# Operand building of each token in three steps, woven around the next token's normalisation

## The chip, the cores and the metric

The kernel runs on one core of a Trainium2 chip. The metric is the device time of one execution in microseconds, the median over several runs. The kernel before took 969.36 us (three runs, 968.85 to 971.9). The engines are TensorE (PE, its weight loads PEld), VectorE (DVE), ScalarE (ACT), GpSimd (POOL) and SyncE (SP), which issues most DMAs. Each engine works through its own list in order.

## The reference

One encoder layer over 768 tokens (a sequence of 512 and one of 256) of width 1024, all in float32. The part around the change is this:

```python
mix = jnp.concatenate([y_rg, y_ml], axis=-1).astype(x.dtype)
x = x + jnp.matmul(mix, w_out)
h = rmsnorm(x, norm2_g)              # y = x * rsqrt(mean(x*x) + EPS) * g
uv = dwconv(jnp.matmul(h, w_up), ffn_conv_w, ffn_conv_b, FFN_CONV // 2, FFN_CONV // 2)
gate, val = jnp.split(uv, 2, axis=-1)
x = x + jnp.matmul(jax.nn.gelu(gate) * val, w_down)
```

Ahead of it come an RMSNorm, the input projection, a gated linear recurrence (channels 0 to 511 of `mix`) and an mLSTM (channels 512 to 1023); behind it only the final RMSNorm.

## The kernel before

Every large product is computed from high and low parts: an operand is rounded to the matmul's format (high), the residue is kept (low), and three matmuls are summed: high times high, low times high, high times low. ScalarE writes the high parts by a copy, VectorE or GpSimd the low ones by a subtraction.

The 768 tokens are six tiles of 128, here called tokens 0 to 5. The output projection is done in two halves of the contraction. The first half (lines 856 to 864) uses the recurrence's channels and adds into `x2`, two tiles of 512 columns per token. The second half is the loop over `PTOK` = 0, 3, 1, 4, 2, 5 at lines 1046 to 1065, which the change rewrites. One pass does, for token c:

1. twelve matmuls for columns 0 to 511 of the projection (`mm_list`, four k-slices times three parts) into a PSUM bank of tag b;
2. `evac`: VectorE adds the bank to `x2`; `square`: ScalarE squares the result and sums each row;
3. `mix_T` for the next token: four transposes into a bank of tag c, a ScalarE copy (`mth`) and a VectorE subtraction (`mtl`);
4. `early`: a piece of preparing the first up-projection weights (`hi_g`, `pair`, `lo_g0`);
5. twelve matmuls for columns 512 to 1023; after the eighth of them `norm2_back` of the token of the pass before: eight transposes of its normalised rows `xn` into two banks of tag c, and the building of operands from them;
6. `evac` and `square` for the second half, then `norm2_front`: `tok_rstd` (a ScalarE Sqrt and small VectorE operations) and two VectorE operations that write `xn` = x times rstd times `g2p`. `g2p` is the gain vector, held in two PSUM banks of tag g;
7. `x2_spill`: the token's rows go to DRAM, on SP's queue.

The up-projection is done by a seven-product scheme on 2 by 2 blocks (Strassen's, in Winograd's form): tokens 0 to 2 against tokens 3 to 5, first against second half of the width. So operand building needs token c - 3 when it comes to token c. For tokens 0 to 2, `norm2_back` writes operands 1 and 2 and keeps two copies `xq`. For tokens 3 to 5 it also forms t1 to t3 on VectorE (two of them read PSUM), t4 on GpSimd, and the high and low parts of operands 3 to 7 (`put_hi` on ScalarE; `put_lo` on GpSimd, or mostly on VectorE for the very last token, whose `norm2_back` is called at line 1215 after the third product). `put_hi(4)` reads t4.

All five engines run in the order of the program in this stage (lines 67 and 868), so where a call stands decides what stands behind it in an engine's list. The tiles `xn`, `xq`, `tq`, `sq`, `mth`, `mtl`, `x2` and the mLSTM's `h` share one pool of 22 slots (`stile`, line 554). The PSUM pool of the stage has tags g (two banks), c (three) and b (three), laid out in the order of their first use; the next pool, `ps8`, has five banks b and three banks c, and its first product is `prod(bd, w, 7, ...)` at line 1212. A tile of a new pool waits for the tiles that had its place (`reuse_waits="tile"`).

After the stage, `window` runs 23 times over up-projection, convolution and gating, and then comes the down-projection.

Of the kernel before, what the change touches and what calls it, by code (L numbers as in the profile page):

```python
# [15 lines left out]
P = 128  # L16
# [17 lines left out]
def kernel(  # L34
# [519 lines left out]
    def stile(name):  # L554
        return mlp["p"].tile([P, 516], F32, tag="s", name=name)
# [279 lines left out]
    def square(c, i, xx, n, j_):  # L835
        if i == 0:
            sums[c] = tiny.tile([P, 4], F32, tag="s2", name="s2")
        A.activation(j_[:, 0:n], xx, AF.Square, accum_out=sums[c][:, i : i + 1])  # L838
# [3 lines left out]
    def tok_rstd(c):  # L842
        s2 = sums.pop(c)
        pre = tiny.tile([P, 3], F32, tag="pre", name="pre")
        V.tensor_scalar(pre[:, 0:1], s2[:, 0:1], 1.0 / D, EPS, op0=MUL, op1=ADD)
        last = s2[:, 1:2]
        rt = tiny.tile([P, 3], F32, tag="rt", name="rt")
        A.activation(rt[:, 0:1], last, AF.Sqrt, bias=pre[:, 0:1], scale=1.0 / D)
        V.tensor_scalar(pre[:, 2:3], last, 1.0 / D, pre[:, 0:1], op0=MUL, op1=ADD)
        V.tensor_scalar(pre[:, 2:3], pre[:, 2:3], -0.5, None, op0=MUL)  # L850
        V.reciprocal(rt[:, 1:2], rt[:, 0:1])
        V.tensor_scalar(rt[:, 2:3], rt[:, 1:2], rt[:, 1:2], pre[:, 2:3], op0=MUL, op1=MUL)
        V.tensor_scalar(rt[:, 0:1], rt[:, 2:3], 1.5, rt[:, 1:2], op0=ADD, op1=MUL)
        return rt[:, 0:1]
# [20 lines left out]
    def bank():  # L875
        return pm["p"].tile([P, 512], F32, tag="b", name="b", bufs=pm["b"])

    def cbank(name):
        return pm["p"].tile([P, 512], F32, tag="c", name=name, bufs=3)
# [70 lines left out]
    def put_hi(i, o, x):  # L950
        A.activation(r32(hilo(i, o)[0]), quad(x), AF.Copy)  # L951

    def put_lo(i, o, x, eng):
        hi, lo = hilo(i, o)
        eng.tensor_tensor(r32(lo), quad(x), hi, op=SUB)

    def mix_T(c):
        ps = cbank("mt")
        for h in range(4):
            PE.transpose(ps[:, h * P : (h + 1) * P], hml[c][:, h * P : (h + 1) * P], ident[:])  # L960
        th, tl = stile("mth"), stile("mtl")
        A.activation(r32(th[:, 0:512]), ps[:], AF.Copy)
        V.tensor_tensor(r32(tl[:, 0:512]), ps[:], th[:, 0:512], op=SUB)
        return th, tl
# [2 lines left out]
    gb = rawtile("g2b")  # L967
    nc.sync.dma_start(gb[:, 0:D], g2.to_broadcast([P, D]))
    sets[0].load_v()
    gbp = [pm["p"].tile([P, 512], F32, tag="g", name="g2p", bufs=2) for _ in range(2)]  # L970
    for hf in range(2):
        A.activation(gbp[hf][:], gb[:, hf * 512 : hf * 512 + 512], AF.Copy)

    def norm2_front(c):
        rr = tok_rstd(c)
        xs = []
        for hf in range(2):
            xn = stile("xn")
            V.scalar_tensor_tensor(xn[:, 0:512], x2[c][hf][:, 0:512], rr, gbp[hf][:], op0=MUL, op1=MUL)  # L979
            xs.append(xn)  # L980
        return xs

    def x2_spill(c):
        for hf in range(2):
# [1 line left out]

    xq = {}

    def norm2_back(c, xs):
        ps = []  # L990
        for hf in range(2):
            ps.append(cbank("tr"))
            for h in range(4):
                PE.transpose(ps[hf][:, h * P : (h + 1) * P], xs[hf][:, h * P : (h + 1) * P], ident[:])
        if c < 3:
            xq[c] = [stile("xq"), stile("xq")]
            for hf in range(2):
                put_hi(1 + hf, c * P, ps[hf])
            put_lo(1, c * P, ps[0], V)
            A.activation(xq[c][1][:, 0:512], ps[1][:], AF.Copy)  # L1000
            A.activation(xq[c][0][:, 0:512], ps[0][:], AF.Copy)
            put_lo(2, c * P, xq[c][1], G)
            return
        o = (c - 3) * P
        x11, x21 = xq.pop(c - 3)
        p12, p22 = ps
        x22 = stile("xq")
        t1, t2, t3, t4 = (stile("tq")[:, 0:512] for _ in range(4))
        A.activation(x22[:, 0:512], p22[:], AF.Copy)
        V.tensor_tensor(t1, p12[:], x11[:, 0:512], op=SUB)  # L1010
        V.tensor_tensor(t3, x22[:, 0:512], p12[:], op=SUB)
        V.tensor_tensor(t2, p22[:], t1, op=SUB)
        put_hi(5, o, t1)
        put_hi(7, o, t3)
        put_hi(6, o, t2)
        put_hi(3, o, p22)
        if c == PTOK[-1]:
            put_lo(5, o, t1, V)
            put_lo(7, o, t3, V)
            put_lo(6, o, t2, V)  # L1020
            V.tensor_tensor(t4, x21[:, 0:512], t2, op=SUB)
            put_hi(4, o, t4)
            put_lo(3, o, p22, V)
            put_lo(4, o, t4, G)
        else:
            put_lo(3, o, x22, G)
            G.tensor_tensor(t4, x21[:, 0:512], t2, op=SUB)
            put_hi(4, o, t4)
            for i, t in ((5, t1), (7, t3), (6, t2), (4, t4)):
                put_lo(i, o, t, G)  # L1030

    def mm_list(ps, acts, hf):
        n = [0]
        for k in range(4):
            (ah, al), (wh, wl) = acts[k], us[k]
            for i, (a, w) in enumerate(((ah, wh), (al, wh), (ah, wl))):
                PE.matmul(ps[:, 0:512], lhsT=a, rhs=w[:, hf * 512 : hf * 512 + 512],  # L1037
                          start=k == 0 and i == 0, stop=k == 3 and i == 2)
                yield

    mt = {PTOK[0]: mix_T(PTOK[0])}
    fr = {}
    u0 = sets[0]
    early = {0: lambda: (u0.hi_g(), u0.sums()), 1: lambda: (u0.pair(0),), 2: lambda: (u0.pair(1),),
             3: lambda: (u0.lo_g0(),), 4: lambda: (), 5: lambda: ()}
    for n, c in enumerate(PTOK):
        th, tl = mt.pop(c)
        acts = [(r32(th[:, i * P : i * P + P]), r32(tl[:, i * P : i * P + P])) for i in range(4)]
        ps = bank()
        for _ in mm_list(ps, acts, 0):  # L1050
            pass
        square(c, 0, evac(c, 0, ps), 512, stile("sq"))
        if n + 1 < NT:
            mt[PTOK[n + 1]] = mix_T(PTOK[n + 1])
        early[n]()
        ps = bank()
        for q, _ in enumerate(mm_list(ps, acts, 1)):
            if q == 7 and n:
                norm2_back(PTOK[n - 1], fr.pop(PTOK[n - 1]))
        square(c, 1, evac(c, 1, ps), 512, stile("sq"))  # L1060
        fr[c] = norm2_front(c)
        if n:
            x2_spill(PTOK[n - 1])
        if n == 4:
            sets[1] = UpSet(1)
# [146 lines left out]
    prod(bd, w, 7, True, 0, cut)  # L1212
    prod(ba, w, 1)
    prod(bb, w, 6, True, 0, cut)
    norm2_back(PTOK[-1], fr.pop(PTOK[-1]))
    u0.hi_22()
    u0.lo_22()()
    mlstack.close()
# [204 lines left out]
```

## Time and profile before

| | |
|---|---|
| median of three runs | 969.36 us |
| the profiled execution | 970.04 us, span 968.3 us |
| PE busy / PEld busy | 95% / 86% of the span |
| VectorE, ScalarE, GpSimd busy | 65%, 52%, 42% |
| granted TensorE clock, mean | 0.978 |
| chain that ended last | PE 73%, DVE 15%, ACT 4%, issue 3%, POOL 3%, DMA 2% |

The profile also cuts the span into 40 slices of 24.2 us. A digit is the busy share of a slice in tenths; PEclk is the granted TensorE clock in tenths:

```profile
PE   8897999999898998799999999999999899999997
POOL 4621433266453326396676676676672000010001
PEclk9898999999999898899999999999999999999999
```

The loop over the six tokens runs from 337 to 393 us of the span, slices 13 to 16 counted from 0, and the first products follow it. From slice 18 on TensorE is busy in nearly all of every slice. The lists of the engines and the waits between them are read from the trace in the section on the rows.

### The profile page before, as it was taken

Reading aid. Unit: us, or ns where it says so; the run is one execution under the profiler, and the core shown is the slowest. Engines: PE = TensorE matmul, PEld = TensorE weight load, DVE = VectorE, ACT = ScalarE, POOL = GpSimd, SP = SyncE. Lnnn points to the kernel's source line nnn. Section 1 sums busy time; section 2 is a strip of 40 time slices with the busy share of each in tenths; the row PEclk is TensorE's granted clock in tenths of the full one; section 3 lists DMA queues with packets and bytes.
Section 4 is the critical chain, followed back from the end, with each engine's and each line's share of the span. In section 5 each row is a group of like instructions: output and inputs, shape, how many; then the busy total and the mean of one; then the engine's idle time right before and its main releaser. Section 6 shows DMA issues by size and latency. Waiting matters only on the chain.

```text
span 968.3 us, 13652 instructions
## 1 busy us (share of the span) xinstructions
PE 916.3 (95%) x5066; PEld 835.3 (86%) x5066; DVE 631.4 (65%) x1176; ACT 500.3 (52%) x826; POOL 404.1 (42%) x261
## 2 busy tenths in 40 slices
PE   8897999999898998799999999999999899999997
PEld 7796877898897776799999999999999788888885
DVE  7678999437869554567667667667677664346523
ACT  6463565154454154476657657667565453326523
POOL 4621433266453326396676676676672000010001
PEclk9898999999999898899999999999999999999999
DMA  6411111042335112142232232331321596527811
GB/s 223 143 56 45 44 66 44 18 149 88 88 104 200 45 56 76 44 148 92 89 120 80 101 120 68 113 120 60 120 77 47 196 344 245 171 82 264 312 40 66
DMA packets 42419, 110.47 MB, mean 114 GB/s; under 512 B 4976, under 2 KB 12656, under 8 KB 42352
## 3 DMA queue, kind: packets, MB, share of 16 engines
q1 hardware_dynamic: 40320, 106.38, 32.5%
q10 hardware_dynamic: 2032, 3.22, 0.9%
q8 instruction: 40, 0.66, 0.3%
q14 instruction: 27, 0.22, 0.1%
HBM read 93.78 MB, written 15.79 MB: 113 GB/s over the span
## 4 chain that ended last, share of the span: by engine, by line
PE 73%; DVE 15%; ACT 4%; issue 3%; POOL 3%; DMA 2%; SPq 0%; POOLq 0%; ACTq 0%; DVEq 0%
PE b L1080 34%; PE d L1313 20%; PE big L141 6%; PE sm L832 3%; PE sm L742 3%; PE sm L451 2%; DVE xc L350 1%; PE b L1037 1%; POOL w_lo L107 1%; DVE thi L386 1%; DVE xgl L252 1%; DMA w_raw<-in_w_down_dram 1%; DVE rs L199 1%; DVE nt L197 1%; ACT hq L951 1%
## 5 line engine op out<-in xcount | busy, mean ns | idle before, releaser
L1080 PE MATMUL b<-hq,w_sh 128*128 128x384 f32 (+2 forms) x792 | 200.1, 335 | 4.4 <-DVE xn L979 3.5
L1313 PE MATMUL d<-w_hi,act 128*128 128x512 f32 x576 | 181.0, 396 | 2.9 <-DVE vl L1126 2.0
L925 POOL TENSOR_TENSOR w_sl<-w_S,w_sh 128x1024 fp32r<-128x1024 f32 x48 | 115.6, 2409 | 120.1 <-ACT w_sh L924 120.1
L1080 PEld LDWEIGHTS b<-hq,w_sh 128*128 128x128 f32 x792 | 143.3, 189 | 5.2 <-issue 4.0
L1313 PEld LDWEIGHTS d<-w_hi,act 128*128 128x128 f32 x576 | 108.6, 189 | 29.0 <-DVE vl L1126 2.5
L1080 PE MATMUL b<-hq,w_sl 128*128 128x384 f32 (+2 forms) x396 | 132.4, 334 | 0.0
L106 ACT ACTIVATE w_hi<-w_raw 128x1024 fp32r<-128x1024 f32 (+1 forms) x77 | 81.0, 1056 | 94.2 <-PE d L1313 57.0
L107 POOL TENSOR_TENSOR w_lo<-w_raw,w_hi 128x1024 fp32r<-128x1024 f32 (+1 forms) x29 | 74.9, 2592 | 122.4 <-ACT w_hi L106 74.9
L1313 PE MATMUL d<-w_lo,act 128*128 128x512 f32 x288 | 113.4, 394 | 0.0
L1080 PE MATMUL b<-hq,w_gh 128*128 128x384 f32 x384 | 98.7, 338 | 0.0
L1289 POOL TENSOR_TENSOR z<-xr,fgb 128x512 f32<-128x512 f32 x6 | 7.8, 1294 | 215.2 <-ACT sq L838 128.4
L107 DVE TENSOR_TENSOR w_lo<-w_raw,w_hi 128x1024 fp32r<-128x1024 f32 x48 | 58.8, 1225 | 58.5 <-ACT w_hi L106 56.9
L1080 PEld LDWEIGHTS b<-hq,w_sl 128*128 128x128 f32 x396 | 75.0, 189 | 0.0
L1080 PEld LDWEIGHTS b<-hq,w_gh 128*128 128x128 f32 x384 | 69.9, 188 | 0.0
L1313 PEld LDWEIGHTS d<-w_lo,act 128*128 128x128 f32 x288 | 54.5, 189 | 12.3
L1080 PE MATMUL b<-hq,w_gl 128*128 128x384 f32 x192 | 64.8, 338 | 0.0
L1108 ACT ACTIVATE cv<-vl,col 128x512 f32<-128x512 f32 (+1 forms) x48 | 32.1, 669 | 49.1 <-DVE vl L1204 47.9
L141 PE MATMUL big<-xgh,w_hi 128*128 128x512 f32 x208 | 54.8, 344 | 2.5 <-DVE kT L762 2.3
L1080 PE MATMUL b<-hq,w_v 128*128 128x384 f32 x288 | 54.4, 337 | 1.0 <-DVE wv L1235 1.0
L141 PE MATMUL big<-xgl,w_hi 128*128 128x512 f32 x208 | 53.3, 337 | 0.0
L141 PE MATMUL big<-xgh,w_lo 128*128 128x512 f32 x208 | 53.3, 337 | 0.0
L1080 PEld LDWEIGHTS b<-hq,w_v 128*128 128x128 f32 x288 | 50.7, 188 | 1.1 <-ACT w_gh L906 1.1
(299 smaller groups left out, 2068.6 us busy)
## 6 DMA issues: line engine op xcount, KB each, us to landing
w_raw<-in_w_down_dram SPq DMA_DIRECT2D x48, 512.0 KB, 4.4
w_g<-in_w_up_dram SPq DMA_DIRECT2D x24, 512.0 KB, 4.1
w_v<-in_w_up_dram SPq DMA_DIRECT2D x24, 512.0 KB, 4.9
actd<-vl SPq DMA_DIRECT2D x24, 384.0 KB, 2.6
a_raw<-actd SPq DMA_DIRECT2D x48, 192.0 KB, 4.5
w_raw<-in_w_fm_dram SPq DMA_DIRECT2D x13, 512.0 KB, 3.4
w_raw<-in_w_out_dram SPq DMA_DIRECT2D x8, 512.0 KB, 5.4
M<-md SPq DMA_DIRECT2D x12, 256.0 KB, 4.2
```

What stands on the lines that cost most here:

```text
L106: A.activation(r32(hi), raw[:, 0:n], AF.Copy)
L107: (V if key[0] == "down" else G).tensor_tensor(r32(lo), raw[:, 0:n], hi, op=SUB)
L141: PE.matmul(dst, lhsT=w, rhs=x[:, lo:hi], start=first and i == 0, stop=last and i == 2,)
L197: V.tensor_tensor(t[:], y, y, op=MUL)
L199: V.scalar_tensor_tensor(y, t[:], 1.5, y, op0=ADD, op1=MUL)
L451: PE.matmul(ps[:, 0:n], lhsT=x[:, p0 : p0 + P], rhs=w[:, o : o + n], start=k == 0 and i == 0, stop=k == 7 and i == 2)
L742: PE.matmul(ps[:, 0:256], lhsT=x[:, p0 : p0 + P], rhs=w[:, o : o + 256], start=n == 0, stop=n == 23)
L832: PE.matmul(ps[:, 0:512], lhsT=a, rhs=w[:, hf * 512 : hf * 512 + 512], start=first and k == 0 and i == 0, stop=last and k == n - 1 and i == 2)
L925: G.tensor_tensor(r32(sl[:, 0:1024]), x, sh[:, 0:1024], op=SUB)
L1080: PE.matmul(t[:, a:b], lhsT=wt, rhs=r32(hq[:, k, off + a : off + b]), start=first and n == 0, stop=n == len(seq) - 1, skip_group_check=True)
L1108: A.activation(t[:, 0 : hi - lo], x[:, lo:hi], AF.Identity, bias=fb[:, m : m + 1], scale=fw[:, 48 + m : 49 + m])
L1313: PE.matmul(bk[c, hf], lhsT=r32(x[:, c * P : c * P + P]), rhs=w[:, hf * 512 : hf * 512 + 512], start=k == 0 and i == 0, stop=k == 23 and i ...
```

## The change

`norm2_front` goes into the loop, and `norm2_back` is split into `norm2_T` (the transposes) and two generators, `back_a` for tokens 0 to 2 and `back_b` for tokens 3 to 5. A generator is advanced in steps: once before the second `evac`, once after the second `square`, and to its end after `xn` is written. The transposes come after ten matmuls of the second half (after eight in the last pass) in place of eight. `mix_T` of the next token moves ahead of the first `square`. Among GpSimd's residues the one of operand 3 moves from ahead of t4 to the end. A bank of tag b is taken first, then `mix_T` takes tag c, and the copies into `g2p` (tag g) follow; an extra one-column Sqrt on ScalarE stands behind them.

```diff
-    gbp = [pm["p"].tile([P, 512], F32, tag="g", name="g2p", bufs=2) for _ in range(2)]
-    for hf in range(2):
-        A.activation(gbp[hf][:], gb[:, hf * 512 : hf * 512 + 512], AF.Copy)
...
+    def norm2_T(c, xs):
         ps = []
         for hf in range(2):
             ps.append(cbank("tr"))
             for h in range(4):
                 PE.transpose(ps[hf][:, h * P : (h + 1) * P], xs[hf][:, h * P : (h + 1) * P], ident[:])
-        if c < 3:
-            xq[c] = [stile("xq"), stile("xq")]
-            for hf in range(2):
-                put_hi(1 + hf, c * P, ps[hf])
-            put_lo(1, c * P, ps[0], V)
-            A.activation(xq[c][1][:, 0:512], ps[1][:], AF.Copy)
-            A.activation(xq[c][0][:, 0:512], ps[0][:], AF.Copy)
-            put_lo(2, c * P, xq[c][1], G)
-            return
+        return ps
...
+    def back_a(c, ps):
+
+        xq[c] = [stile("xq"), stile("xq")]
+        put_hi(1, c * P, ps[0])
+        yield
+        put_lo(1, c * P, ps[0], V)
+        put_hi(2, c * P, ps[1])
+        yield
+        A.activation(xq[c][1][:, 0:512], ps[1][:], AF.Copy)
+        A.activation(xq[c][0][:, 0:512], ps[0][:], AF.Copy)
+        put_lo(2, c * P, xq[c][1], G)
+        yield
+
+    def back_b(c, ps, last):
+
         o = (c - 3) * P
         x11, x21 = xq.pop(c - 3)
         p12, p22 = ps
         x22 = stile("xq")
         t1, t2, t3, t4 = (stile("tq")[:, 0:512] for _ in range(4))
         A.activation(x22[:, 0:512], p22[:], AF.Copy)
+        yield
         V.tensor_tensor(t1, p12[:], x11[:, 0:512], op=SUB)
+        put_hi(5, o, t1)
+        yield
         V.tensor_tensor(t3, x22[:, 0:512], p12[:], op=SUB)
         V.tensor_tensor(t2, p22[:], t1, op=SUB)
-        put_hi(5, o, t1)
         put_hi(7, o, t3)
         put_hi(6, o, t2)
         put_hi(3, o, p22)
-        if c == PTOK[-1]:
+        if last:
...
         else:
-            put_lo(3, o, x22, G)
             G.tensor_tensor(t4, x21[:, 0:512], t2, op=SUB)
             put_hi(4, o, t4)
-            for i, t in ((5, t1), (7, t3), (6, t2), (4, t4)):
+            for i, t in ((5, t1), (7, t3), (6, t2), (4, t4), (3, x22)):
                 put_lo(i, o, t, G)
+        yield
...
+    first = bank()
     mt = {PTOK[0]: mix_T(PTOK[0])}
+    gbp = [pm["p"].tile([P, 512], F32, tag="g", name="g2p", bufs=2) for _ in range(2)]
+    for hf in range(2):
+        A.activation(gbp[hf][:], gb[:, hf * 512 : hf * 512 + 512], AF.Copy)
+    A.activation(pre[:], ones[:, 0:1], AF.Sqrt)
...
-        ps = bank()
+        ps = bank() if n else first
         for _ in mm_list(ps, acts, 0):
             pass
-        square(c, 0, evac(c, 0, ps), 512, stile("sq"))
+        xx = evac(c, 0, ps)
         if n + 1 < NT:
             mt[PTOK[n + 1]] = mix_T(PTOK[n + 1])
+        square(c, 0, xx, 512, stile("sq"))
         early[n]()
         ps = bank()
+        back = iter(())
         for q, _ in enumerate(mm_list(ps, acts, 1)):
-            if q == 7 and n:
-                norm2_back(PTOK[n - 1], fr.pop(PTOK[n - 1]))
+            if q == (9 if n < 5 else 7) and n:
+                p = PTOK[n - 1]
+                tr = norm2_T(p, fr.pop(p))
+                back = back_a(p, tr) if p < 3 else back_b(p, tr, False)
+        next(back, None)
         square(c, 1, evac(c, 1, ps), 512, stile("sq"))
-        fr[c] = norm2_front(c)
+        next(back, None)
+        rr = tok_rstd(c)
+        fr[c] = []
+        for hf in range(2):
+            xn = stile("xn")
+            V.scalar_tensor_tensor(xn[:, 0:512], x2[c][hf][:, 0:512], rr, gbp[hf][:], op0=MUL, op1=MUL)
+            fr[c].append(xn)
+        for _ in back:
+            pass
...
-    norm2_back(PTOK[-1], fr.pop(PTOK[-1]))
+    for _ in back_b(PTOK[-1], norm2_T(PTOK[-1], fr.pop(PTOK[-1])), True):
+        pass
```

## Rows read from the trace of the kernel before

**Rows 1.** The page's first part: busy us, share of the span, instructions.

```profile
PE 916.3 (95%) x5066; PEld 835.3 (86%) x5066; DVE 631.4 (65%) x1176; ACT 500.3 (52%) x826; POOL 404.1 (42%) x261
```

**Rows 2.** Waits from 337 to 416 us: us in total, times, longest.

```profile
PE tr L994 <- DVE xn L979: 7.3, 2, 3.9
```

**Rows 3.** Timeline of PE, turn 2: start, us, operation, count [idle before <-releaser].

```profile
352.10 0.40 PE L1037 MATMUL b<-w_lo,mth 128*128 128x512 f32 x1
...
353.74 0.39 PE L1037 MATMUL b<-w_lo,mth 128*128 128x512 f32 x1
...
355.83 0.39 PE L1037 MATMUL b<-w_lo,mth 128*128 128x512 f32 x1
...
358.13 0.39 PE L1037 MATMUL b<-w_hi,mtl 128*128 128x512 f32 x1
...
359.51 0.39 PE L1037 MATMUL b<-w_hi,mth 128*128 128x512 f32 x1
```

**Rows 4.** Timeline of PE, turns 3 and 5 and first products.

```profile
365.99 0.40 PE L1037 MATMUL b<-w_hi,mtl 128*128 128x512 f32 x1
370.30 1.94 PE L994 MATMUL tr<-ident,xn 128*128 128x128 f32 x8 [3.91 <-DVE xn L979]
...
375.83 0.39 PE L1037 MATMUL b<-w_lo,mth 128*128 128x512 f32 x1
...
386.01 0.40 PE L1037 MATMUL b<-w_hi,mtl 128*128 128x512 f32 x1
...
392.81 0.40 PE L1037 MATMUL b<-w_lo,mth 128*128 128x512 f32 x1
396.71 0.77 PE L1080 MATMUL b<-hq,w_sh 128*128 128x256 f32 x2 [3.49 <-DVE xn L979]
...
399.41 0.64 PE L1080 MATMUL b<-hq,w_gh 128*128 128x384 f32 x2
...
401.65 0.40 PE L1080 MATMUL b<-hq,w_sh 128*128 128x256 f32 x2
...
403.08 1.04 PE L994 MATMUL tr<-ident,xn 128*128 128x128 f32 x8
```

**Rows 5.** Timelines of ACT, DVE and POOL, end of turns 4 and 5.

```profile
386.54 0.63 ACT L951 ACTIVATE hq<-tq 128x512 fp32r<-128x512 f32 x1 [2.66 <-POOL tq L1027]
387.08 0.61 ACT L838 ACTIVATE sq<-x 128x512 f32<-128x512 f32 x1
...
393.98 0.63 ACT L838 ACTIVATE sq<-x 128x512 f32<-128x512 f32 x1 [0.37 <-DVE x L824]
...
394.73 0.29 ACT L848 ACTIVATE rt<-s,pre 128x1 f32<-128x1 f32 x1
...
393.25 0.69 DVE L824 TENSOR_TENSOR x<-b,x 128x512 f32<-128x512 f32 x1 [0.38 <-PE b L1037]
...
395.81 1.41 DVE L979 SCALAR_TENSOR_TENSOR xn<-x,rt,g2p 128x512 f32<-128x512 f32 x2
...
385.22 1.30 POOL L1027 TENSOR_TENSOR tq<-xq,tq 128x512 f32<-128x512 f32 x1
386.47 4.94 POOL L955 TENSOR_TENSOR hq<-tq,hq 128x512 fp32r<-128x512 f32 x4
```

**Rows 6.** Timeline of ACT in turn 0.

```profile
343.02 0.63 ACT L838 ACTIVATE sq<-x 128x512 f32<-128x512 f32 x1 [4.38 <-DVE x L824]
...
347.00 1.28 ACT L848 ACT_TABLE_LOAD   x1
```

**Rows 7.** PE after two waits, and windows there (third last column: granted clock).

```profile
257.84 0.68 PE L589 MATMUL sm<-vw,ktok 128*128 128x129 f32 x4 [3.17 <-DVE h L661]
...
315.15 0.79 PE L832 MATMUL sm<-w_hi,mh 128*128 128x512 f32 x1 [3.19 <-DVE x L824]
...
258.80:260.80 2.00, 2.00 (x20) 2.00 (x19) 0.44 (x2) 0.00 (x0) 0.00 (x0) 1.00 0.96 229
316.00:318.00 2.00, 2.00 (x6) 1.52 (x6) 2.00 (x7) 0.00 (x0) 0.00 (x0) 0.50 0.41 137
```

More of the change, by code (lines that the diff above doesn't have):

```diff
@@ L969 @@
     sets[0].load_v()
-    gbp = [pm["p"].tile([P, 512], F32, tag="g", name="g2p", bufs=2) for _ in range(2)]
-    for hf in range(2):
-        A.activation(gbp[hf][:], gb[:, hf * 512 : hf * 512 + 512], AF.Copy)
-    def norm2_front(c):
-        rr = tok_rstd(c)
-        xs = []
-        for hf in range(2):
[L978 to L984, printed above, removed]
-            nc.sync.dma_start(x2d[c, :, hf * 512 : hf * 512 + 512], x2[c][hf][:, 0:512])
-    xq = {}
-    def norm2_back(c, xs):
+    def norm2_T(c, xs):
         ps = []
@@ L994, in norm2_back, with x2_spill @@
                 PE.transpose(ps[hf][:, h * P : (h + 1) * P], xs[hf][:, h * P : (h + 1) * P], ident[:])
-        if c < 3:
-            xq[c] = [stile("xq"), stile("xq")]
-            for hf in range(2):
-                put_hi(1 + hf, c * P, ps[hf])
-            put_lo(1, c * P, ps[0], V)
-            A.activation(xq[c][1][:, 0:512], ps[1][:], AF.Copy)
-            A.activation(xq[c][0][:, 0:512], ps[0][:], AF.Copy)
-            put_lo(2, c * P, xq[c][1], G)
-            return
+        return ps
+    def x2_spill(c):
+        for hf in range(2):
+            nc.sync.dma_start(x2d[c, :, hf * 512 : hf * 512 + 512], x2[c][hf][:, 0:512])
+    xq = {}
+    def back_a(c, ps):
[10 more added lines that the diff above has]
+    def back_b(c, ps, last):
         o = (c - 3) * P
@@ L1048 @@
         acts = [(r32(th[:, i * P : i * P + P]), r32(tl[:, i * P : i * P + P])) for i in range(4)]
-        ps = bank()
+        ps = bank() if n else first
         for _ in mm_list(ps, acts, 0):
             pass
-        square(c, 0, evac(c, 0, ps), 512, stile("sq"))
+        xx = evac(c, 0, ps)
         if n + 1 < NT:
             mt[PTOK[n + 1]] = mix_T(PTOK[n + 1])
+        square(c, 0, xx, 512, stile("sq"))
         early[n]()
         ps = bank()
+        back = iter(())
         for q, _ in enumerate(mm_list(ps, acts, 1)):
-            if q == 7 and n:
-                norm2_back(PTOK[n - 1], fr.pop(PTOK[n - 1]))
-        square(c, 1, evac(c, 1, ps), 512, stile("sq"))
-        fr[c] = norm2_front(c)
+            if q == (9 if n < 5 else 7) and n:
[3 more added lines that the diff above has]
+        next(back, None)
+        square(c, 1, evac(c, 1, ps), 512, stile("sq"))
+        next(back, None)
+        rr = tok_rstd(c)
+        fr[c] = []
+        for hf in range(2):
+            xn = stile("xn")
[3 more added lines that the diff above has]
+            pass
         if n:
```

## The prediction, made before the changed kernel ran

> **What bounds the kernel now.** The engine table comes first: TensorE is busy in 95% of the span, so only time in which it waits or runs slowly can be won [rows 1]. The 40 slices show where that is: this stage lies in slices 14 to 16, where PE and its clock dip. The waits of the stage come next: TensorE's transposes waited 7.3 us in two places for the normalised token xn [rows 2]. The timeline of TensorE then gives the price of each dip, as time beyond what its matmuls need. The need is read from a quiet turn [rows 3]: nine steps from 353.74 to 355.83 are 0.232 us each; eight steps and the four transposes of mix_T take 2.30 (355.83 to 358.13), so these transposes cost 0.44; two steps and the eight transposes of norm2 take 1.38 (358.13 to 359.51), so these cost 0.92.
>
> I call the passes of the token loop turns 0 to 5 (tokens 0, 3, 1, 4, 2, 5). Five places lose time:
> - S1, S2: at the head of turn 2, three steps take 1.64 (352.10 to 353.74) where 0.70 would do [rows 3]. 0.94 is lost; turn 3 begins with the same pattern.
> - S3: in turn 3, ten steps and the eight transposes take 9.84 (365.99 to 375.83) where 3.24 would do: 6.60 lost, 3.91 of it waiting [rows 4], the rest at the lower clock.
> - S4: the same in turn 5, four steps and the transposes: 6.80 (386.01 to 392.81) against 1.85, 4.95 lost [rows 4].
> - S5: from the last matmul of turn 5 to the first product, 3.90 (392.81 to 396.71) against 0.23, 3.67 lost; then the first half product takes 2.70 (396.71 to 399.41) where the third, of the same shape, takes 1.43 (401.65 to 403.08): 1.27 for the clock [rows 4].
>
> Together 2 x 0.94 + 6.60 + 4.95 + 3.67 + 1.27 = 18.4 us. That is all this change could win here.
>
> The timelines of the other engines say why. In turns 2 and 4 ScalarE's in-order queue holds put_hi(4), which waits 2.66 us for t4 from GpSimd, and the token's second square stands right behind it (386.54, 387.08) [rows 5]. GpSimd computes t4 only after the residue put_lo(3) and takes 1.26 for it (385.22 to 386.47). So xn of turns 2 and 4 is late, and the next turn's transposes are what meets it: S3 and S4. S5 is another thing: the first product's bank is the one that held the first half of g2p, because tag g was the first tag of the old PSUM pool; it starts at 396.71, when the first of the two xn of 395.81 to 397.22 is done and the second isn't [rows 4, 5]. The wait therefore goes by tile, not by pool.
>
> **The change, part by part.**
>
> *Tag order.* Tag b now takes the first three banks, c the next, g the last two. The first three products of the new pool fall on old b banks, emptied long before. S5's wait on xn goes; token 5's transposes, which need xn anyway, come after three products. The two g2p copies now follow the first mix_T on ScalarE, which was idle for 4.38 us before the first square [rows 6]; they are 512-wide copies like the 0.63 of rows 5, so 1.3 at most. The Sqrt activation adds one tiny instruction and pulls the table load of 1.28 [rows 6] into the same gap: 2.9 with its 0.29 [rows 5], inside 4.38. Cost nothing; without that cover the load would sit in token 0's normalisation, as it does now.
>
> *mix_T before square.* The copy of mt no longer waits for the evacuation and the square. S1 and S2 go in turn 2. In turn 3 the same spot gets a new wait (N1 below).
>
> *Back in three steps.* The second square now stands ahead of everything that waits for GpSimd. From the evacuation (393.25) to the square is 0.73, to Sqrt 0.75 more, to xn 1.08 more [rows 5]: 2.56; one put_hi put in between adds 0.54 (386.54 to 387.08). So xn starts 3.10 us after the evacuation starts, and the evacuation 0.44 after the last matmul's start (392.81 to 393.25). xn is ready 3.54 + 1.41 = 4.95 after that matmul, and the transposes after ten matmuls of the next turn's second half come 22 steps and a mix_T later, 5.6 us: no wait. In turn 5, with no mix_T and q = 7, it is 20 steps, 4.6, and the first half of xn (4.25) suffices. S3 and S4 go.
>
> *What is late next.* t3 and t2 now come after xn on VectorE, then t4 on GpSimd, then put_hi(4), and behind that in ScalarE's queue stands mix_T's copy for turn 4, with VectorE's mtl behind it.
> - N1, head of turn 4: last matmul of turn 2 to mtl done: 4.95 + 2 x 0.69 (t3, t2, the shape of 393.25) + 1.26 (t4) + 0.54 (put_hi(4)) + 0.60 (mth, a 512-wide copy) + 0.69 (mtl) + 0.1 for hand-overs = 9.5. TensorE needs 26 steps + 0.44 + 0.92 = 7.4 to its second matmul of turn 4. 2.1 lost, in pieces under 1.4. The second-half transposes of turn 3 also wait about 0.9 for put_hi(3) to free their bank; that lies inside the same 2.1.
> - N2, first product: put_lo(7) of token 4 is the second of five residues of 1.24 (4.94 for four [rows 5]) after t4. Last matmul of turn 4 to there: 4.95 + 1.38 + 1.26 + 2 x 1.24 = 10.1. TensorE needs 25 steps + 0.92 + 0.2 = 6.9. 3.2 lost, then perhaps the low clock: 1.27, as in S5.
> - Walked in the same way, token 2's high half and residue of operand 1 are ready about 3.2 us after the end of turn 5's matmuls on ScalarE and VectorE; the second product needs them 4.7 after. Token 5's xn is ready by 6 us, its transposes come after 8. No wait.
>
> After token 5's transposes every engine has the same list as now, so the later time moves as a whole; GpSimd's last residue of token 2 ends about 2 us before that. SP's queue keeps its order: spills, then set 1's two loads; the first still waits for lo_g0, which GpSimd now does after five residues, much when it does now, and its user comes over 15 us later.
>
> **The clock in N2.** Two waits of nearly one length ended differently here: after 3.17 us the granted clock was 1.00 (2.4 GHz), after 3.19 us it was 0.50 (1.2 GHz) [rows 7]. N2 can go either way. Both ends: 0 and 1.27; I take 1.27, since S5, 3.49 us before the very same product, paid it [rows 4].
>
> The Trainium skill (TensorE: Matmul & The Clock Gate, "HAM oscillation") holds that a gap shorter than a limit it names keeps the clock up; that would keep it in N2, 1.27 us better than the sum here. The trace agrees with it for one of the two waits of rows 7 and not for the other.
>
> **Sum.** 18.4 - 2.1 - 3.2 - 1.27 = 11.8 us. The profiled execution took 970.04 us (span 968.3); the median of the runs is 969.36, 0.7 below it. From the median: 957.5 us.
>
> **Rivals.**
> - *A, the 22 slots of the token pool.* With t1 to t4 alive over the next normalisation, all 22 are in use in turn 2 (ten x2, two h, mth and mtl, x21, x22, t1 to t4, two xn), and turn 3's new tiles take slots that GpSimd is still reading. If the second square of turn 3 gets the last one, it waits until t4 + 5 x 1.24: about 3.8 late, of which xn has 2.0 to spare, 1.8 lost: 959.3. If mth gets it, 5.6 + 2.7 (S3's slow part, 6.60 - 3.91): 965.8. Against it: what the transposes wait for now is xn [rows 2], and no wait of the stage's list is one for a slot. The Trainium skill (Perfetto Trace Analysis, "Optimization Strategy") names too few buffers as one cause of repeated bubbles; no row here shows that yet.
> - *B, the tag order doesn't do what it says.* If the first product's bank still belongs to g2p, it starts with the first xn of token 5, 2.2 us after N2 would let it: 959.7. For: which bank a tag gets is not visible in any row. Against: the wait by tile in S5.
> - *C, slower.* N1's broken stretch brings the clock down and it stays at 1.2 GHz until the first set is through. Half products took 2.70 and 1.43 at the two levels, a factor of 1.89. From turn 3's transposes to token 5's TensorE has 50 steps (11.6), one 0.44, three 0.92 and 5.1 of products (two of 1.43, one of 2.24), 19.9; at the low clock 17.7 more, while N2 (3.2 + 1.27) hides behind it; two more products (3.7) add 3.3. 957.5 + 17.7 - 4.5 + 3.3 = 974.0. It turns slower than before once some 18 us of TensorE's work run low without a break. Against: in S3 the clock was back after 5.5 us of steady work (375.83 follows at full rate).
>
> **Chances.** Forecast 0.60, A 0.18, B 0.08, C 0.04; 0.10 for what I haven't seen (0.04 still faster, 0.05 with the win eaten, 0.01 slower). About 0.3% is what a measurement here tells from no change. Faster by more: 0.60 + 0.18 + 0.08 + 0.04 = 0.90; within: 0.05; slower: C's 0.04 + 0.01 = 0.05. Range: 953.0 (no clock loss, and N2 mostly gone because one of its hand-overs is shorter) to 964.0 (A near its hard end).
>
> **What would show it.** Right: no wait of TensorE above 1 us for xn; a short broken stretch at the head of turn 4 behind mth and mtl; the first product's second matmul waiting some 3 us for a residue of GpSimd; token 5's transposes 11 to 13 us earlier. Wrong: transposes still waiting for xn (weaving doesn't help), squares or mth that start when a GpSimd residue ends (A), the first product starting with xn (B), a clock of 0.5 over more than 6 us (C), or a stage shorter by 12 and a span that isn't: then the later stage was bound by something else.

## The result, and the profile after

The changed kernel took 954.78 us (median of four runs, 952.73 to 955.7). The kernel before took 969.11 beside it (966.04 to 971.9). The ratio is 0.985, with a 95% interval of 0.9816 to 0.9884. The forecast was 957.5 in a range of 953 to 964. The profiled execution has a span of 953.1 us.

The first part of the page, as in [rows 1]: the same 5066 matmuls are now busy for 908.2 us instead of 916.3. The work is the same, and the mean granted clock is 0.986 instead of 0.978, so I take the 8.1 us for time that TensorE had run at the low clock, in the whole span.

```profile
PE 908.2 (95%) x5066; PEld 828.5 (87%) x5066; DVE 631.4 (66%) x1176; ACT 500.4 (53%) x827; POOL 403.9 (42%) x261
```

The waits of the stage, as in [rows 2] (engine, line, what it waited for: us in total, times, longest). The 7.3 us for xn are gone. A residue on GpSimd has come in their place.

```profile
PE b L1096 <- POOL hq L955: 2.7, 1, 2.7
PE b L1035 <- ACT mth L962: 1.0, 2, 0.7
...
PE tr L976 <- ACT hq L951: 0.8, 1, 0.8
```

The timeline of PE, which answers to [rows 3, 4] (start, us, operation, count, [idle before <- releaser]): turn 3's transposes and the head of turn 4, then the first products and token 5's transposes.

```profile
363.69 0.60 PE L976 MATMUL tr<-ident,xn 128*128 128x128 f32 x4
...
365.11 0.66 PE L976 MATMUL tr<-ident,xn 128*128 128x128 f32 x4 [0.81 <-ACT hq L951]
...
366.52 0.50 PE L1035 MATMUL b<-w_hi,mth 128*128 128x512 f32 x1 [0.29 <-ACT mth L962]
...
367.58 0.40 PE L1035 MATMUL b<-w_lo,mth 128*128 128x512 f32 x1
...
380.50 0.39 PE L1035 MATMUL b<-w_lo,mth 128*128 128x512 f32 x1
...
380.73 0.28 PE L1096 MATMUL b<-hq,w_sh 128*128 128x256 f32 x1
...
383.66 0.39 PE L1096 MATMUL b<-hq,w_sh 128*128 128x256 f32 x1 [2.66 <-POOL hq L955]
...
385.92 0.84 PE L1096 MATMUL b<-hq,w_gh 128*128 128x384 f32 x2
...
388.69 0.40 PE L1096 MATMUL b<-hq,w_sh 128*128 128x256 f32 x2
...
390.12 1.03 PE L976 MATMUL tr<-ident,xn 128*128 128x128 f32 x8
```

Read it in two places. From 363.69 to 367.58 TensorE issues eight transposes and four steps (a step is one 128x512 matmul), which need 0.92 + 4 x 0.232 = 1.85; it takes 3.89, so 2.04 are lost (N1). From 380.50 to 385.92 it issues one step and one half product, 0.23 + 1.43; it takes 5.42, so 3.76 are lost, and the second product (385.92 to 388.69) takes 2.77 instead of 2.24, another 0.53. N2 is thus 4.29 with its clock.

The timelines of ACT, DVE and POOL, as in [rows 5, 6], show why:

```profile
338.78 1.28 ACT L1044 ACT_TABLE_LOAD   x1
...
363.34 1.23 ACT L951 ACTIVATE hq<-tq 128x512 fp32r<-128x512 f32 x2 [2.83 <-DVE tq L1010]
...
365.35 0.63 ACT L951 ACTIVATE hq<-tq 128x512 fp32r<-128x512 f32 x1 [0.29 <-POOL tq L1024]
...
365.88 0.58 ACT L962 ACTIVATE mth<-mt 128x512 fp32r<-128x512 f32 x1
...
361.30 1.41 DVE L1074 SCALAR_TENSOR_TENSOR xn<-x,rt,g2p 128x512 f32<-128x512 f32 x2
...
362.62 0.68 DVE L1010 TENSOR_TENSOR tq<-xq,tr 128x512 f32<-128x512 f32 x1
...
363.22 0.68 DVE L1011 TENSOR_TENSOR tq<-tr,tq 128x512 f32<-128x512 f32 x1
...
364.05 1.27 POOL L1024 TENSOR_TENSOR tq<-xq,tq 128x512 f32<-128x512 f32 x1 [3.46 <-DVE tq L1011]
...
381.12 4.98 POOL L955 TENSOR_TENSOR hq<-tq,hq 128x512 fp32r<-128x512 f32 x4
```

The table load now lies in the idle stretch ahead of the first square (338.78, before 347.00 [rows 6]). At the end of turn 2 VectorE computes xn first (361.30), then t3 and t2 (362.62, 363.22), for which ScalarE has idled 2.83 us at 363.34. GpSimd's t4 follows at 364.05, put_hi(4) at 365.35 and the high mixing tile right behind it at 365.88, for which the matmul at 366.52 waits. In turn 5 the residues of token 4 start at 381.12 at 1.245 each; the second of them, put_lo(7), ends at 383.6, and the matmul at 383.66 starts there. The windows (third last column: granted clock) show what follows that wait:

```profile
360.00:368.00 8.00, 6.67 (x33) 4.87 (x32) 5.56 (x13) 4.62 (x11) 4.54 (x5) 1.00 0.16 62
383.66:387.40 3.74, 3.74 (x16) 3.74 (x17) 2.47 (x8) 1.51 (x4) 3.74 (x4) 0.54 0.31 124
387.40:391.00 3.60, 3.60 (x30) 3.60 (x29) 0.17 (x1) 0.00 (x0) 1.19 (x1) 1.00 0.00 0
```

The broken stretch around N1 kept 2.4 GHz; the 2.66 us of N2 brought 1.2 GHz for most of 3.7 us.

**Where the time went.** I measure every kernel from three starts of the PE timeline: the first transposes of mix_T, token 5's transposes, and the first matmul of the down-projection. "The stage" below is the first stretch.

| | before | changed | difference |
|---|---|---|---|
| start of the stage | 337.41 | 336.52 | 0.89 |
| the stage | 65.67 | 53.60 | 12.07 |
| from there to the down-projection | 353.45 | 353.40 | 0.05 |
| down-projection, first to last matmul | 204.21 | 201.99 | 2.22 |

The last row isn't the change's. The lists are the same there, and in the profile of before one wait was long and the clock was low behind it (changed kernel: 1.08 us at 753.27):

```profile
766.97 0.73 PE L1313 MATMUL d<-w_hi,act 128*128 128x512 f32 x2 [2.05 <-DVE vl L1126]
```

In the twelve experiments this stretch took 201.55 to 202.31 us, also in those that are almost the kernel before. Likewise the stage starts anywhere from 334.49 to 340.17 us though the work ahead of it is the same. So the times of two single executions can differ by 5 us and more for nothing, while the stage came out at 53.60 and 53.67 in two profiles of the changed kernel. I therefore read small effects from the stage, not from the time.

### The profile page after: what moved, and what is told of

It reads as the page before. It is cut to its first block, busy times and chain, and to the rows that moved or that the text cites. A ratio compares the mean times of both kernels' runs of the same rounds, so it can differ in the third digit from the quotient of the medians.

```text
span 953.1 us, 13653 instructions
## 1 busy us (share of the span) xinstructions
PE 908.2 (95%) x5066; PEld 828.5 (87%) x5066; DVE 631.4 (66%) x1176; ACT 500.4 (53%) x827; POOL 403.9 (42%) x261
## 4 chain that ended last, share of the span: by engine, by line
PE 73%; DVE 16%; POOL 3%; ACT 3%; issue 2%; DMA 2%; SPq 0%; POOLq 0%; ACTq 0%; DVEq 0%
PE b L1096 34%; PE d L1330 20%; PE big L141 6%; PE sm L832 3%; PE sm L742 3%; PE b L1035 2%; DVE xc L350 2%; PE sm L451 1%; DVE w L375 1%; POOL hq L955 1%; POOL w_lo L107 1%; DVE thi L386 1%; DVE nt L197 1%; DVE xgl L252 1%; DVE rs L199 1%
## 5 line engine op out<-in xcount | busy, mean ns | idle before, releaser
L107 DVE TENSOR_TENSOR w_lo<-w_raw,w_hi 128x1024 fp32r<-128x1024 f32 x48 | 58.8, 1225 | 56.3 <-ACT w_hi L106 55.2
```

The lines of the kernel that those rows point to most:

```text
L107: (V if key[0] == "down" else G).tensor_tensor(r32(lo), raw[:, 0:n], hi, op=SUB)
```

## The experiments

My theory after the result: the forecast's terms are right, but which part of the change earns which term isn't shown. The rival for each: another part does it, or something else is late next. All kernels in one view, sorted by stage (the ratios are to runs of the kernel before on the same chip, medians 966.73, 967.1 and 967.59; a single run gives no interval):

| kernel | stage, us | median, us (runs) | ratio to before, 95% |
|---|---|---|---|
| before | 65.67 | 969.11 (4) | |
| e1, tag order alone | 61.24 | 962.08 (6) | 0.9936 to 0.997 |
| e3, residue of 3 last, alone | 60.78 | 961.92 (7) | 0.994 to 0.9969 |
| e12, not woven, old residue order | 58.48 | 957.69 (1) | |
| e2, changed, old tag order | 56.43 | 957.14 (4) | 0.9885 to 0.9928 |
| e8, mixing late and no preload | 55.58 | 958.82 (1) | |
| e10, mixing late | 54.42 | 956.4 (1) | |
| e11, no preload | 53.90 | 956.1 (1) | |
| e6, residue of 7 first | 53.73 | 953.67 (4) | 0.9824 to 0.9898 |
| e4, changed again | 53.67 | 956.14 (6) | 0.9871 to 0.9914 |
| the changed kernel | 53.60 | 954.78 (4) | 0.9816 to 0.9884 |
| e7, tail held back | 52.48 | 953.69 (4) | 0.9829 to 0.9905 |
| e5, not woven | 51.61 | 954.09 (4) | 0.9819 to 0.9893 |
| e9, tail held back, early copy | 48.84 | 950.43 (5) | 0.9796 to 0.9848 |

**Tag order: e1 and e2.** e1 is the kernel before with only the new order of tags (below). e2 is the changed kernel with the old one: the two lines of gbp stand ahead of mix_T, and no bank is taken first.

```diff
+    first = bank()
     mt = {PTOK[0]: mix_T(PTOK[0])}
+    gbp = [pm["p"].tile([P, 512], F32, tag="g", name="g2p", bufs=2) for _ in range(2)]
+    for hf in range(2):
+        A.activation(gbp[hf][:], gb[:, hf * 512 : hf * 512 + 512], AF.Copy)
...
-        ps = bank()
+        ps = bank() if n else first
```

> The kernel before with the new tag order alone (bank b first, then mix_T's bank, then the copies into g2p; no early Sqrt). The stage from the first mix_T to token 5's transposes takes 65.7 us before and 53.6 in the changed kernel. Theory (the first product waits for xn because its bank held g2p): S3 and S4 stay as they are, the wait of 3.5 us ahead of the first product goes; S5's slow part (1.27) goes only if S4's low clock has ended by then. Stage 60.8 to 62.0, time 4 to 5 us below before, 964 to 965. Rival (the wait goes by pool, or the bank is another's): the first product still starts with the first half of xn, stage 65.7, time unchanged.

> The changed kernel with the old tag order (g2p copies first, as before). Theory: in the changed kernel the first product is held by the residue put_lo(7) anyway, until 383.7 in its trace; with the old tags it waits for the first half of token 5's xn, ready at about 385.7. So the tag order is worth only some 2 us here, not the 4.9 of S5: stage 55.6 to 56.4, time 2 to 3 us above the changed kernel. Rival (the tag order is worth S5 in any company): 4.9 us above it, stage 58.5.

e1: the first product no longer waits, and 4.43 us of the stage are gone (S5 was 4.94). The transposes still wait, 3.88 and 3.90 us for xn. e2: the first product waits for token 5's xn again, at its first matmul, as in [rows 4]:

```profile
386.60 0.76 PE L1095 MATMUL b<-hq,w_sh 128*128 128x256 f32 x2 [4.99 <-DVE xn L1073]
```

But the stage is only 2.8 us longer than in the changed kernel, not 4.9: with the old tags this wait covers the residue that otherwise costs N2. The tag order does what the forecast said; in company it is worth 2.8 of its 4.9. (The median of e2 is 1.0 above that of e4, on the same chip; that is within what the times differ by.)

**The changed kernel again: e4.** No edit.

> The changed kernel once more, to size it against before on one chip. Of the 15.2 us between the two profiles 12.1 lie in the stage, 0.9 ahead of it and 2.2 at the head of the down-projection, where the lists of the engines are the same. Theory (those 3.1 are scatter of loads and of the clock): stage 53.6 within 0.5, time 11 to 14 us below before; the wait at the head of the down-projection differs from the last profile's. Rival (the change also helps there): 14 to 16 us below, with the down-projection's head as in the last profile of the changed kernel (waits of 0.7 and 1.1, no clock loss).

956.14 us, 0.9871 to 0.9914: 10.6 us below the kernel before, just short of the 11 to 14 expected. The wait at the head of the down-projection was 0.9 us, near the 1.08 of the last profile, so it doesn't tell theory and rival apart. That the 2.2 us there are scatter rests on e1 and e3, which have the lists of the kernel before and took 202.31 and 202.14. The two intervals of the changed kernel overlap (0.9871 to 0.9884); a gain of some 12 us lies in both.

**What took S3 and S4 away: e3, e5, e12.** e3 is the kernel before with one line moved. e5 is the changed kernel with the operands of a token built in one piece, ahead of the second square, as before. e12 is e5 with the two lines of e3 the other way round, so that the residue of operand 3 is first again. First e3's edit, then e5's:

```diff
-            put_lo(3, o, x22, G)
             G.tensor_tensor(t4, x21[:, 0:512], t2, op=SUB)
             put_hi(4, o, t4)
-            for i, t in ((5, t1), (7, t3), (6, t2), (4, t4)):
+            for i, t in ((5, t1), (7, t3), (6, t2), (4, t4), (3, x22)):
```

```diff
-        next(back, None)
+        for _ in back:
+            pass
         square(c, 1, evac(c, 1, ps), 512, stile("sq"))
-        next(back, None)
```

> The kernel before with one line moved: GpSimd's residue of operand 3 after t4 and the other residues, as in the changed kernel; nothing woven. Theory (S3 and S4 come from put_hi(4) waiting for t4 ahead of the second square): t4 follows t2 or GpSimd's weight residue directly; put_hi(4) 1.8 us earlier in turn 2, 2.5 in turn 4. S3's wait falls from 3.9 to about 2.1, S4's from 3.4 to about 0.9 with the clock staying up; stage 65.7 down to 57 to 61, time 5 to 9 us below before. Rival (the weaving is what counts, the normalisation is too long behind all of the back's work): both waits shorten by less than 1 us, time within 2 us of before.

> The changed kernel with the three steps run in one piece ahead of the second evacuation and square, as before; tag order, mix_T ahead of square, transposes after ten matmuls, early Sqrt and the residue of operand 3 at the end stay. Theory A (a walk along the queues of the changed trace): square stands behind put_hi(4) again, but t4 now follows t2 at once. xn of turn 2 comes some 3 us later and turn 3's transposes wait 1.3; turn 5's wait 1.4; in exchange t2 and the residues come 4 to 5 us earlier, so the wait for put_lo(7) ahead of the first product (2.7 and the low clock) goes. Stage 50 to 52 against 53.6, time 1.5 to 3.5 us below the changed kernel. Rival (the weaving is what removes S3 and S4, as the prediction has it): both waits return at 3 us or more with their low clock, stage 58 or more.

> The kernel of e5_unwoven (operands in one piece ahead of the second square) with the residue of operand 3 first again, ahead of t4, as in the kernel before: of the change there remain the tag order, the mixing transposes ahead of the square, the preload and the transposes two steps later. It asks which of the changed parts took the waits for the normalised tile out of turns 3 and 5. Theory (the place of t4 in GpSimd's queue did, since put_hi(4) and behind it the second square wait for it): t4 comes 1.26 us later, the two waits of 1.52 and 1.91 us grow to 2.8 and 3.2, and the stage lasts at least 51.61 + 2.5 = 54.1 us, up to 59.5 where each wait also brings the low clock (2.7 each, as in turn 3 before). Rival (the later transposes and the earlier mixing tiles did most of it, so that the residue order matters little): waits below 2.2 us, stage under 52.6.

The timelines of PE: e3, e5 and e12.

```profile
367.54 1.28 PE L994 MATMUL tr<-ident,xn 128*128 128x128 f32 x8 [2.09 <-DVE xn L979]
...
384.27 1.29 PE L994 MATMUL tr<-ident,xn 128*128 128x128 f32 x8 [1.73 <-DVE xn L979]
```

```profile
366.20 1.29 PE L976 MATMUL tr<-ident,xn 128*128 128x128 f32 x8 [1.52 <-DVE xn L1074]
...
381.44 1.28 PE L976 MATMUL tr<-ident,xn 128*128 128x128 f32 x8 [1.91 <-DVE xn L1074]
```

```profile
365.17 1.94 PE L976 MATMUL tr<-ident,xn 128*128 128x128 f32 x8 [3.34 <-DVE xn L1075]
...
383.73 1.94 PE L976 MATMUL tr<-ident,xn 128*128 128x128 f32 x8 [3.93 <-DVE xn L1075]
```

One moved line (e3) cuts the two waits from 3.91 and 3.39 to 2.09 and 1.73 and the stage by 4.9, although the first product then waits longer (4.21). The second wait had been expected at 0.9, and the time, 4.8 below the kernel before, just misses the 5 to 9. Without the weaving (e5) the waits are 1.52 and 1.91 (1.3 and 1.4 expected), the stage is *shorter* than in the changed kernel by 2.0 us, and neither N1 nor N2 is there. In this profile 0.4 of the 2.0 is lost again behind the stage (last section), and the times don't show the rest: 954.09 against 954.78 and 956.14. With the old residue order as well (e12) S3 and S4 are back, 3.34 and 3.93 us and the low clock (0.50 from 365.17 to 368.20), and the stage is 6.9 longer. So, as long as the second square stands behind put_hi(4), most of the waits of [rows 2] hang on the place of t4 in GpSimd's queue. The timelines of ACT and POOL in e12 show the chain, with e5's rows behind them:

```profile
361.92 0.63 ACT L951 ACTIVATE hq<-tq 128x512 fp32r<-128x512 f32 x1 [2.65 <-POOL tq L1025]
...
359.35 1.29 POOL L955 TENSOR_TENSOR hq<-xq,hq 128x512 fp32r<-128x512 f32 x1 [0.53 <-ACT hq L951]
...
360.59 1.29 POOL L1025 TENSOR_TENSOR tq<-xq,tq 128x512 f32<-128x512 f32 x1
```

```profile
362.95 0.63 ACT L951 ACTIVATE hq<-tq 128x512 fp32r<-128x512 f32 x1 [0.82 <-POOL tq L1024]
...
361.63 1.29 POOL L1024 TENSOR_TENSOR tq<-xq,tq 128x512 f32<-128x512 f32 x1
```

In e12 GpSimd first waits for put_hi(3) (0.53), computes that residue (1.24) and only then t4; ScalarE waits 2.65 for t4 with the square behind it. In e5 t4 goes ahead, and ScalarE waits 0.82: 1.8 less, more than the 1.26 I had expected, since GpSimd's own wait goes too. The forecast did name this chain, but gave its end to the weaving. Whether the weaving would remove S3 and S4 with the old residue order wasn't run, and neither was the change without the later place of the transposes (after ten matmuls).

**Mixing transposes and preload: e8, e10, e11.**

The first edit is e10's, the second e11's; e8 has both.

```diff
         xx = evac(c, 0, ps)
+        square(c, 0, xx, 512, stile("sq"))
         if n + 1 < NT:
             mt[PTOK[n + 1]] = mix_T(PTOK[n + 1])
-        square(c, 0, xx, 512, stile("sq"))
```

```diff
-    A.activation(pre[:], ones[:, 0:1], AF.Sqrt)
```

> The changed kernel with mix_T behind the first square again and without the early Sqrt. Theory (S1 came from both: the table load in token 0's normalisation delays the evacuation, and the copy of mt stood behind square): 0.7 us lost again at the head of turn 2, and 0.6 more at the head of turn 4; stage 54.7 to 55.2 against 53.6. Rival (one of them alone, or neither, matters): no wait at the head of turn 2; stage 53.6 to 54.3.

> The changed kernel with the mixing transposes and their evictions again behind the first square of a token (their place before the change), the Sqrt preload kept. Beside the run that left out the preload as well (stage 55.58 us) and the changed kernel (53.6) this splits the two. Theory (the later place of the mixing tiles' evictions is the larger part): waits for the high mixing tile come back at the heads of turns 3 and 4 and the stage lasts 54.2 to 55 us. Rival (the table load inside the first turn was what cost): stage 53.6 to 53.9, no new wait.

> The changed kernel without the Sqrt preload alone, the mixing transposes where the change has them. Theory (the table load then falls between the first token's squares and its square root, where only the first normalised tile waits for it, and that one has cover): stage 53.6 to 54.0 us. Rival (the load of 1.28 us delays the second turn's tiles): stage 54.5 to 55, with a new wait at the head of turn 1 or 2.

The timeline of PE in e8:

```profile
353.92 0.50 PE L1035 MATMUL b<-w_hi,mth 128*128 128x512 f32 x1 [0.26 <-ACT mth L962]
...
370.35 0.51 PE L1035 MATMUL b<-w_hi,mth 128*128 128x512 f32 x1 [0.91 <-ACT mth L962]
```

S1 (head of turn 2) is back only when both are undone; with either in place it is gone. It costs more than expected: at turn 3's transposes e8 is 1.05 us behind the changed kernel, and its stage, 55.58, lies above the 54.7 to 55.2. With the late place alone (e10) 0.7 of the 0.8 us lies at the head of turn 4, where the wait for the high mixing tile grows from 0.29 to 0.90; the waits that I expected at the head of turn 3 didn't come. Without the preload alone (e11) no wait is new, and the 0.2 to 0.3 us are hardly more than two profiles of one kernel differ by. S2 came back in none of the three, so neither edit is needed to remove it. In e1 and e3 it is still there, so neither the tag order nor the residue order removes it alone; which part did wasn't singled out.

**What is late next: e6, e7, e9.** e6 computes the residue of 7 first. e7 keeps the weaving but holds put_hi(4) and the residues that nobody needs yet until the next turn's first square (for token 4, until token 5's xn is done). e9 moves one copy in e7.

```diff
-            for i, t in ((5, t1), (7, t3), (6, t2), (4, t4), (3, x22)):
+            for i, t in ((7, t3), (6, t2), (5, t1), (4, t4), (3, x22)):
```

e7, in back_b for tokens 3 and 4 (token 5 keeps the old lines), and in the loop:

```diff
         put_hi(5, o, t1)
         yield
-        V.tensor_tensor(t3, x22[:, 0:512], p12[:], op=SUB)
-        V.tensor_tensor(t2, p22[:], t1, op=SUB)
-        put_hi(7, o, t3)
-        put_hi(6, o, t2)
-        put_hi(3, o, p22)
+            put_hi(3, o, p22)
+            V.tensor_tensor(t3, x22[:, 0:512], p12[:], op=SUB)
+            V.tensor_tensor(t2, p22[:], t1, op=SUB)
+            put_hi(7, o, t3)
+            put_hi(6, o, t2)
+            if c == 3:
+                G.tensor_tensor(t4, x21[:, 0:512], t2, op=SUB)
+            put_lo(7, o, t3, G)
+            put_lo(6, o, t2, G)
+            if c > 3:
+                G.tensor_tensor(t4, x21[:, 0:512], t2, op=SUB)
+            put_lo(5, o, t1, G)
+            yield
...
-            G.tensor_tensor(t4, x21[:, 0:512], t2, op=SUB)
             put_hi(4, o, t4)
-            for i, t in ((5, t1), (7, t3), (6, t2), (4, t4), (3, x22)):
+            for i, t in ((4, t4), (3, x22)):
...
         square(c, 0, xx, 512, stile("sq"))
+        if n < 5:
+            for _ in tail:
+                pass
...
+        if n == 5:
+            for _ in tail:
+                pass
-        for _ in back:
-            pass
+        if n in (2, 4):
+            next(back, None)
+            tail = back
+        else:
+            for _ in back:
+                pass
```

e9, in back_a:

```diff
+        if c == 2:
+            A.activation(xq[c][0][:, 0:512], ps[0][:], AF.Copy)
         put_hi(2, c * P, ps[1])
         yield
         A.activation(xq[c][1][:, 0:512], ps[1][:], AF.Copy)
-        A.activation(xq[c][0][:, 0:512], ps[0][:], AF.Copy)
+        if c != 2:
+            A.activation(xq[c][0][:, 0:512], ps[0][:], AF.Copy)
```

> The changed kernel with the residues in the order 7, 6, 5, 4, 3 in place of 5, 7, 6, 4, 3. Theory (N2 is the wait of the first product for put_lo(7), second in GpSimd's list): the wait falls by one residue, 1.24, from 2.7 to 1.4, and the clock then stays up: stage 51.1 to 52.4 against 53.6, time 1 to 2.5 us below the changed kernel. Rival (another operand is late as well, or the list of GpSimd doesn't decide): stage as in the changed kernel.

> The changed kernel with three more moves in the operand building of tokens 3 and 4: put_hi(3) right behind put_hi(5); residues 7 and 6 first (for token 4 ahead of t4); put_hi(4) with the last residues held until the next turn's first square (token 3) or behind token 5's xn (token 4). Theory (N1 is mix_T's copy behind put_hi(4) and the transposes behind put_hi(3); N2 is put_lo(7) behind t4 and residue 5): N1 falls from 2.0 to 0.5, N2 from 2.7 to 0.3 with the clock up; stage 48 to 49.5 against 53.6, time 4 to 6 us below the changed kernel. Rival (operand 1 of token 2 or another input of the first products is late next): the waits move, stage 51 or more.

> The kernel of e7_held_tail with one copy moved: for token 2 the copy of the first transposed half (it is the last reader of the bank that the second product of the four takes over) goes ahead of the high part of operand 2, so it runs at about 381 us instead of 383.30 to 383.89. Theory (the second product's wait of 2.54 us there was for that copy alone, and nothing else is late next): the wait falls to 0 to 0.5 us, with it most of the low clock behind it, and the stage from the first mixing transposes to token 5's transposes lasts 49 to 50.5 us, 2 to 3.5 less than in e7 (52.48) and 3 to 4.6 less than in the changed kernel (53.60, 53.67); time 950 to 952.5 us against 953.7 in e7. Rival (the wait moves once more, to the residue of operand 2 or 4 on GpSimd or to token 5's normalised tile, which the copy now delays by 0.55 us on ScalarE): the stage stays at 51.5 us or more.

e6 and e7, timelines of PE (for e7 of ACT too):

```profile
381.50 0.39 PE L1096 MATMUL b<-hq,w_sh 128*128 128x256 f32 x1 [1.44 <-POOL hq L955]
...
384.29 1.01 PE L1096 MATMUL b<-hq,w_gh 128*128 128x384 f32 x2 [1.22 <-ACT xq L994]
```

```profile
379.83 0.39 PE L1121 MATMUL b<-hq,w_sh 128*128 128x256 f32 x1 [0.27 <-POOL hq L955]
...
383.94 1.01 PE L1121 MATMUL b<-hq,w_gh 128*128 128x384 f32 x2 [2.54 <-ACT xq L994]
...
383.30 0.59 ACT L994 ACTIVATE xq<-tr 128x512 f32<-128x512 f32 x1
```

In both the wait moved as the rival said. In e6 the residue's wait fell from 2.66 to 1.44, but the second product then waited 1.22 for the copy of token 2's first transposed half, and the stage gained nothing. In e7 one wait of 0.23 is left of N1 and 0.27 of the residue's wait, and that same copy (383.30) costs 2.54 and the low clock. It is the last reader of the bank that the second product takes over. e9 runs it at 380.91. The waits of TensorE from 337 to 420 us, and the rows of PE and ACT:

```profile
PE b L1124 <- DVE wv L1280: 1.0, 1, 1.0
PE b L1052 <- ACT mth L962: 0.7, 1, 0.7
...
PE b L1124 <- POOL hq L955: 0.3, 1, 0.3
```

```profile
381.56 0.61 PE L1124 MATMUL b<-hq,w_gh 128*128 128x384 f32 x2 [0.18 <-ACT xq L992]
...
380.91 0.60 ACT L992 ACTIVATE xq<-tr 128x512 f32<-128x512 f32 x1
```

In the stage nothing above 0.7 us is left, and that 0.7 is at the very start, where it was in every kernel; the wait of 1.0 lies behind the stage, in every kernel too. The stage lasts 48.84 us, just below the 49 to 50.5 expected and 4.8 less than in the changed kernel; the forecast's need, 65.67 - 18.4, is 47.3. Behind the stage 0.4 of the 4.8 is lost again (last section). At 950.43 us e9 is faster than before at 0.9796 to 0.9848. Against the changed kernel that is 4.4 and 5.7 us by the two medians; its interval is clear of the changed kernel's second one (from 0.9871) and overlaps the first (from 0.9816). The stage, 48.84 against 53.60 and 53.67, is the firmer evidence.

## Why the prediction was right, and where it gave the credit wrongly

- **Sum.** 11.8 us were forecast, and the stage is 12.07 shorter. By terms: 18.4 - 2.04 - 4.29 = 12.1. The times differ by 14.3 (969.11 - 954.78), and 954.78 is 2.7 below the forecast: what lies outside the stage is scatter (e4, the table of stretches).
- **N1**: forecast 2.1, measured 2.04, with waits of 0.81, 0.29 and 0.22 in it, in pieces as said, behind put_hi(3) (0.81 against 0.9), mth and mtl.
- **N2**: forecast 3.2 + 1.27, measured 2.8 until the second matmul of the first product (380.50 to 383.66, less a step of 0.23 and 0.12 for one of the half product's twelve matmuls) and 1.5 for the clock, 4.3 together against 4.47. The releaser is put_lo(7), as said.
- **S5 and the tag order**: right. e1 wins 4.43 with it, the first product starts without a wait. Rival B is out.
- **S3 and S4 by weaving**: what was forecast came. xn of turn 2 is ready at 362.71 (361.30 + 1.41), and the transposes start at 363.69 without a wait. What the forecast had wrong is the credit. It lists no part for the moved residue of operand 3, though it names that residue as the cause. e5 has no weaving and keeps only 1.52 + 1.91 us of the waits, and e12, unwoven too, brings S3 and S4 back through GpSimd's order alone. Over the need of 47.3 e5's stage loses 4.3 us, 3.43 of it in these two waits; the woven stage loses 6.3, N1 and N2. With the residue of 3 last the weaving is a loss of 2.0 in the stage. I had worked out N1 and N2 as prices of the whole change and never asked what the change would be without the weaving.
- **S1, S2 by mix_T before square; the preload at no cost**: half right. Both end, but for S1 either edit is enough (e8, e10, e11), and S2 ends without either (e8). The early mixing transposes pay 0.8 us, but elsewhere: mostly at the head of turn 4.
- **The clock in N2**: I took the low one, after the very product of [rows 4], and it came (0.54; in e4, e8, e10 and e11, with waits of 2.65 to 2.68, it came too). My rows left both open, so that it came out right is in part luck. By the Trainium skill (TensorE: Matmul & The Clock Gate, "HAM oscillation") it would have stayed up through a gap this short; the granted clock here disagrees, and the sum by it, 13.1, lies further from the 12.07 than mine.
- **Rivals A and C**: no wait for a slot is in the stage's list, and no square or mth starts with the end of a residue (366.36, the next square, follows mth). The clock was 1.00 over 360 to 368 and again from 387.4. Neither happened.
- **What comes later moves as a whole**: right, 353.45 against 353.40.

## What to carry to other kernels

When a change mixes several edits, work out each price *without* each of the others: here the piece that gave the change its look cost 2.0 us of the stage, and a one-line reordering in GpSimd's queue wins most of what it was credited with. Where an in-order engine waits for a product of a slow one, put that product first in the slow one's queue and everything that nobody awaits last. After each wait that is removed, look for the last reader of the buffer that the next operation takes over: here it was a copy that could run 2.4 us earlier.

## What the hardware showed that I had not expected

How long TensorE waited didn't by itself decide its clock. In this stage the granted clock was 1.00 after single waits of 1.91 us (e5) and 2.09 us (e3), and 0.5 after 2.54 (e7) and 2.66 (changed kernel), though 3.17 us had kept it elsewhere [rows 7]. In e6 it was 0.50 after two waits of 1.44 and 1.22 us, with 1.6 us of work between them. The windows of e6, between and after the two waits:

```profile
381.50:383.00 1.50, 1.50 (x11) 1.36 (x11) 0.88 (x3) 1.50 (x5) 1.50 (x2) 1.00 0.86 287
384.29:387.30 3.01, 3.01 (x9) 3.01 (x10) 1.17 (x2) 0.00 (x0) 3.01 (x3) 0.50 0.00 0
```

Some 9.5 us behind the start of token 5's transposes every kernel waits 0.93 to 1.00 us for one tile of VectorE (wv). Even that short a wait had either level behind it: 0.50 in e1, e5, e9 and e12, 1.00 in the other ten profiles. Here are the row and the window of e9, and the row of e3, where the clock was 1.00 from 406.81 to 410.00:

```profile
394.73 3.84 PE L1124 MATMUL b<-hq,w_v 128*128 128x384 f32 x12 [0.98 <-DVE wv L1280]
394.73:398.55 3.82, 3.82 (x13) 3.82 (x14) 1.75 (x3) 2.75 (x4) 3.66 (x4) 0.55 0.47 191
...
406.81 2.34 PE L1079 MATMUL b<-hq,w_v 128*128 128x384 f32 x12 [1.00 <-DVE wv L1234]
```

The low stretch adds 1.5 us to these twelve matmuls, but the wait behind them, 0.9 us, then goes. From token 5's transposes to the down-projection the four kernels took 353.80 to 353.84 us and the others 353.38 to 353.46: 0.4 more. So halving a wait in front of a second one may win back nothing, as in e6. What separates the waits that kept the clock from those that didn't stays open.
